# Two preparation stages in a chunked delta net: masked scores two blocks ahead, decays and inverses one block ahead

## The chip, the cores and the metric

One core of a Trainium2 chip runs the whole kernel. The metric is the device time of one execution in microseconds; the table below gives the median of three runs. TensorE does the matmuls, VectorE and ScalarE the work on PSUM and SBUF, GpSimd the products that need no PSUM, SyncE issues the transfers.

## The reference

Two layers run over 1040 tokens of 1024 features: a gated delta net, a gated feed-forward layer with a causal convolution, an mLSTM and a second feed-forward layer, each between root-mean-square norms. The change touches the gated delta net only. For each of 16 value heads (two to each of 8 query/key heads) and each chunk it computes

```python
G = cumsum(g)                                   # g: log decays of a chunk
decay = exp(where(i >= j, G[i] - G[j], -inf))
a_mat = I + (beta*k) @ k.T * decay * strict     # strict: below the diagonal
u, w = solve(a_mat, [v*beta, k*beta*exp(G)])
attn = (q @ k.T) * decay
# from chunk to chunk, S the state of a head:
v_new = u - w @ S
o = (q*exp(G)) @ S + attn @ v_new
S = S*exp(G_last) + (k*exp(G_last - G)).T @ v_new
```

Here q and k are the outputs of a projection, a causal convolution of four taps and a SiLU, then divided by their norms; o is normed, multiplied by a gate z, and projected back.

## The kernel before, in words

**Tiling.** The tokens lie along the free dimension, 1044 with padding: three token blocks of 348 (`BS`), each of three chunks of 116 (`CH`). Features lie on the 128 partitions. The delta net walks through 24 blocks, n = 3h + b for query/key head h and token block b. A block has two value heads.

**Projections.** A unit is one tile of 128 output features for one token block: eight k-steps of three matmuls each (`mm3`: high weight by high input, high by low, low by high), 24 matmuls of 128x348. `project(n)` makes two tiles for all three token blocks, six units, 144 matmuls. It yields in the middle and at the end of each unit, so it has twelve steps. With n mod 3 = 0 it makes the two z tiles of head h, with 1 the q and k tiles of head h + 1, with 2 the two v tiles of head h + 1, and ends with a burst of SiLUs on ScalarE between two loads of activation tables. Each unit of q, k or v also has a convolution: a multiply by the norm's factors (L308), one ScalarE pass (L695) and three VectorE passes (L697).

**Preparation** (`gdn_prepare`, L738). First the scores, three steps: the squares of k (L746), their sum over features by two matmuls (`kn`, L274 and L275), its inverse root, k times that (L750); k against k, masked, into `scs_kk`; k against q, masked, into `scs_qk` (`score_block`, L576 and L579, one buffer each). Then for each of the two value heads the decays (`decay_block`: transposed sums L559, `eG` L561, `E` L566 and L567), the masked matrix `ah` (L911) with its rest `A` and `al` on GpSimd (L914, L915), its first level (L912), `att` (L764) and the decayed q (`qd`, L767) on GpSimd. The tiles eG, E and A share three buffers. Then the two inverses in step with each other: Z (L920), X by TensorE (L923) and ScalarE (L924), six doubling levels of three steps each (L949, L958, L963 with L953, L959, L964), a correction (L969 to L977) and the result XT (L979).

**Recurrence** (`gdn_recur`) goes through a block's three chunks with the state S: k, v0 and v1 transposed (L795), k by S (L828), XT by the difference (L839), the new state (L848, L854) and, one chunk later, the outputs (L812, L813). **Finish** (`gdn_finish`) norms and gates a block's outputs and stores them.

**Order.** The kernel is written as generators. `weave` takes steps from several of them in proportion to weights: next comes the one with the smallest (steps done + 0.5) / weight. One `weave` is made for each block n, and the next starts in the program's order only when all its parts are done. The order so written is a priority: a planner orders each engine's instructions by readiness under its own estimates of durations, earlier written ones first, and gives out buffers as it goes. On the chip each engine then runs its own list in that fixed order, with semaphores between engines.

```python
            parts = [(self.gdn_recur(n, tb), 14)]
            if n + 1 < n_all:
                parts.insert(0, (self.gdn_prepare(n + 1, tb, lb), 27))
            if n:
                parts.append((self.gdn_finish(n - 1), 4))
            parts.append((project(n), 8) if n <= n_all - NB else (islice(out, 28), 28))
            weave(*parts)
```

So the preparation of block n + 1, scores included, stands beside the recurrence of block n. The projection has twelve steps at weight 8, so that when the other parts have reached their ends some four of its steps are left. In the last two blocks the steps of the output projection (`out`) take its place.

Of the kernel before, what the change touches and what calls it, by code (L numbers as in the profile page):

```python
# [23 lines left out]
NB = 3  # L24
# [40 lines left out]
def weave(*parts):  # L65

    live = [[g, max(n, 1), 0] for g, n in parts]
    while live:
        p = min(live, key=lambda p: (p[2] + 0.5) / p[1])
        try:  # L70
            next(p[0])
            p[2] += 1
        except StopIteration:
            live.remove(p)


def run(g):
    for _ in g:
        pass


class Trunk:
# [154 lines left out]
    def project(self, w, b, name, rows=P):  # L237

        ps = self.next_bank(f"pj_{name}_{b}")
        for k in range(KD):  # L240
            self.mm3(ps[:rows, :BS], w[k], self.x(k, b), k == 0, k == KD - 1)
        if self.now:
            self.now.pop()()
        return ps[:rows, :BS]
# [361 lines left out]
    def gdn(self):  # L606
        a = self.a
        self.o_dram = [self.pd.tile([P, 2, TP], F32, tag=f"o_g_{h}", name=f"o_g_{h}", bufs=1) for h in range(NQK)]
        self.pages_of = {}
        self.blocks = {}  # L610
        n_all = NQK * NB
        tiles = lambda h: [h, NQK + h, 2 * NQK + 2 * h, 2 * NQK + 2 * h + 1, 32 + 2 * h, 32 + 2 * h + 1]

        def silu(h, tiles):
            self.burst([y for i in tiles for y in self.pages_of[h, i]], self.last, AF.Silu)

        def project(n):


            h, part = divmod(n, NB)  # L620
            i = (4, 0, 2)[part]
            g = h + (part > 0)
            yield from self.gdn_project(g, tiles(g)[i : i + 2], i)
            silu(g, (i, i + 1))

        def enter(b):
            hs = []
            for m in range(KD):
                h = self.page("C", f"hs_in_{b}_{m}", N_PAGES)
                sl = slice(b * BS, (b + 1) * BS)  # L630
                nc.sync.dma_start(h, self.hs[:, m, sl])
                self.put_input(h, m, sl)
                hs.append(h)
            return hs

        nc = self.nc
        t0 = tiles(0)
        weights = lambda t: self.split_weights(a["gdn_w_in"][t], f"gi{t}")
        self.new_input(0, "in")
        self.rt = self.new_factors("in")  # L640
        wg = self.split_weights(a["gdn_gate_w"], "gdn_gates", 32)
        hs = [enter(0)]
        ws = [weights(t0[0])]
        self.tables()
        hs.append(enter(1))
        ws.append(weights(t0[1]))
        hs.append(enter(2))
        rows = []
        for b in range(NB):
            acc = self.squares(hs[b], f"in{b}")  # L650
            self.now.append(lambda acc=acc, b=b: self.norm(acc, f"in{b}", self.r(b)))
            rows.append(self.gate_rows(wg, b, "gdn"))
            if b == NB - 1:
                gates = self.gdn_gates(rows)
                next(gates)
            for i in range(2):
                run(self.gdn_unit(0, i, t0[i], ws[i], b))
        lb, tb = next(gates)
        silu(0, (0, 1))
        order = t0[2:4] + [t for h in range(NQK) for t in tiles(h)[4:] + (tiles(h + 1)[:4] if h + 1 < NQK else [])]  # L660
        self.queue_weights([(a["gdn_w_in"][t], f"gi{t}") for t in order], 1)

        def first():
            yield from self.gdn_project(0, tiles(0)[2:4], 2)
            silu(0, (2, 3))

        weave((self.gdn_prepare(0, tb, lb), 13), (first(), 6))
        out = self.out_projection(a["gdn_w_out"], NQK, "go", GDN_CORE, GDN_LATE, 1, 2)
        for n in range(n_all):
            parts = [(self.gdn_recur(n, tb), 14)]  # L670
            if n + 1 < n_all:
                parts.insert(0, (self.gdn_prepare(n + 1, tb, lb), 27))
            if n:
                parts.append((self.gdn_finish(n - 1), 4))
            parts.append((project(n), 8) if n <= n_all - NB else (islice(out, 28), 28))
            weave(*parts)
        weave((self.gdn_finish(n_all - 1), 4), (out, 30))

# [56 lines left out]
            reason="issue order",  # L735
        )

    def gdn_prepare(self, n, tb, lb):  # L738


        nc, core = self.nc, self.core
        h, b = divmod(n, NB)
        q, k = self.pages_of[h, 0][b], self.pages_of[h, 1][b]
        nm = f"{h}_{b}"
        ksq = self.scratch(f"ksq_{nm}")
        nc.scalar.activation(ksq, k, AF.Square)  # L746
        ps = self.bank("sp", f"kn_{nm}")
        self.over_features(ps[:, :BS], ksq, f"k{nm}")
        rk = self.rstd(ps[:, :BS], 1.0, EPS, f"k{nm}")
        nc.vector.tensor_tensor(k, k, rk, ALU.mult)  # L750
        yield
        kk = self.score_block(k, k, self.m_strict, f"kk{nm}")
        yield
        qk = self.score_block(k, q, self.m_incl, f"qk{nm}")
        yield
        at, qd, invs = [], [], []
        XT = [None, None]
        for i in range(2):
            vh = 2 * h + i
            E, eG = self.decay_block(tb, lb, vh, b, f"{vh}_{b}")  # L760
            invs.append(self.inverse(kk, E, f"{vh}_{b}", i, XT))
            next(invs[i])
            att = core.tile([CH, BS], F32, tag="att", name=f"att_{vh}_{b}", bufs=4)
            nc.gpsimd.tensor_tensor(att, qk, E, ALU.mult)  # L764
            at.append(att)
            qe = core.tile([P, BS], F32, tag="qd", name=f"qd_{vh}_{b}", bufs=4)
            nc.gpsimd.tensor_tensor(qe, q, eG, ALU.mult)  # L767
            qd.append(qe)
            yield
        while invs:  # L770
            for g in list(invs):
                if next(g, 1):
                    invs.remove(g)
            yield
        self.blocks[n] = (at, qd, XT)
# [722 lines left out]
```

## Time and profile before

| | |
|---|---|
| median of 3 runs | 3444.45 us (3444.33 to 3444.45) |
| time of the profiled execution | 3444.23 us |
| its span | 3442.5 us |
| mean granted TensorE clock | 0.969 |
| TensorE busy (matmuls) | 3212.2 us, 93% of the span |
| VectorE busy | 2373.1 us, 69% |
| ScalarE busy | 1609.0 us, 47% |
| GpSimd busy | 1652.2 us, 48% |

The span runs from the first to the last instruction. Matmuls are pipelined and their ends are modelled in the profile, so a busy TensorE is not one at its peak; how far apart matmuls start says more. PE stands for TensorE, PEld for its weight loads, DVE for VectorE, ACT for ScalarE, POOL for GpSimd. A row of a group or of the timeline ends with the idle time of the engine just before it and the instruction that ended that idle time. The granted clock is the share of full speed that TensorE was given.

### The profile page before, as it was taken

The numbers are of one execution on the slowest core, as the hardware profiler recorded it, in microseconds if no ns is written. First come the engines' busy times: TensorE is split into PE (matmuls) and PEld (weight loads), VectorE is DVE, ScalarE is ACT, GpSimd is POOL, SyncE is SP. The second block draws the span as 40 slices with busy tenths as digits, with TensorE's granted clock in tenths as the row PEclk, the third lists the DMA queues.
The fourth block names the chain that finished last, engine by engine and source line by source line (L and its number), as shares of the span: only waits on it lengthen the run. The fifth ranks groups of instructions, "written<-read, shape, count | busy, mean of one in ns | idle before, by whom it ended". The sixth has DMA issues, their size and how long they took to land. (4 is left out here: it accounts for less than half of the span.)

```text
span 3442.5 us, 68429 instructions
## 1 busy us (share of the span) xinstructions
PE 3212.2 (93%) x25368; PEld 3119.6 (91%) x25368; DVE 2373.1 (69%) x5143; ACT 1609.0 (47%) x3390; POOL 1652.2 (48%) x1890
## 2 busy tenths in 40 slices
PE   7999999999999998799999989899998799999998
PEld 6889988988988897799999989899998799999998
DVE  7777777777767649877677484534469867777474
ACT  5455545555545435655455243323345645445232
POOL 2433443444334444577665434333344477666453
PEclk9999999999999999899999999999999899999999
DMA  3011100101001344422224453211125422224452
GB/s 118 23 37 34 34 29 31 34 32 34 31 31 40 107 132 152 134 93 93 78 78 133 133 182 125 93 44 50 56 78 183 136 90 87 87 75 132 132 180 88
DMA packets 234511, 297.75 MB, mean 86 GB/s; under 512 B 20684, under 2 KB 167104, under 8 KB 234176
## 3 DMA queue, kind: packets, MB, share of 16 engines
q1 hardware_dynamic: 234176, 293.37, 26.3%
q8 instruction: 200, 3.28, 0.4%
q14 instruction: 135, 1.11, 0.1%
HBM read 240.06 MB, written 53.23 MB: 85 GB/s over the span
## 5 line engine op out<-in xcount | busy, mean ns | idle before, releaser
L233 PE MATMUL pj_gi<-xh_in,wh_gi 128*128 128x348 f32 x1152 | 394.2, 342 | 5.5 <-ACT wh_gi L137 3.7
L233 PE MATMUL dn_f<-so_f,wh_f 128*128 128x260 f32 x1344 | 386.6, 288 | 11.8 <-ACT wh_f L137 5.0
L235 PE MATMUL pj_gi<-xh_in,wl_gi 128*128 128x348 f32 x1152 | 395.7, 343 | 0.9 <-POOL wl_gi L138 0.9
L234 PE MATMUL pj_gi<-xl_in,wh_gi 128*128 128x348 f32 x1152 | 393.5, 342 | 0.0
L235 PE MATMUL dn_f<-so_f,wl_f 128*128 128x260 f32 x1344 | 384.7, 286 | 0.0
L234 PE MATMUL dn_f<-so_f,wh_f 128*128 128x260 f32 x1344 | 384.5, 286 | 0.0
L138 POOL TENSOR_TENSOR wl_f<-wr_f,wh_f 128x512 fp32r<-128x512 f32 x168 | 226.0, 1362 | 246.0 <-ACT wh_f L137 113.5
L1278 DVE SCALAR_TENSOR_TENSOR z<-u,fcw,z 128x260 f32<-128x260 f32 x528 | 243.4, 487 | 49.8 <-ACT z L1276 35.0
L138 POOL TENSOR_TENSOR wl_u_s<-wr_u,wh_u_s 128x512 fp32r<-128x512 f32 x176 | 228.2, 1300 | 97.7 <-ACT wh_u_s L137 97.3
L233 PEld LDWEIGHTS dn_f<-so_f,wh_f 128*128 128x128 f32 x1344 | 257.7, 192 | 13.6 <-ACT z L1276 5.5
L441 DVE TENSOR_TENSOR acc_f<-acc_f,dn_f 128x260 f32<-128x260 f32 x320 | 133.1, 421 | 189.2 <-PE dn_f L235 188.2
L234 PEld LDWEIGHTS dn_f<-so_f,wh_f 128*128 128x128 f32 x1344 | 258.2, 192 | 0.2
L235 PEld LDWEIGHTS dn_f<-so_f,wl_f 128*128 128x128 f32 x1344 | 258.2, 192 | 0.1
L1276 ACT ACTIVATE z<-u,fcb,fcw 128x260 f32<-128x260 f32 x352 | 192.3, 570 | 93.7 <-DVE u L196 92.4
L233 PEld LDWEIGHTS pj_gi<-xh_in,wh_gi 128*128 128x128 f32 x1152 | 222.1, 193 | 8.0 <-ACT wh_gi L137 4.0
L235 PEld LDWEIGHTS pj_gi<-xh_in,wl_gi 128*128 128x128 f32 x1152 | 222.6, 193 | 2.4 <-POOL wl_gi L138 1.2
L234 PEld LDWEIGHTS pj_gi<-xl_in,wh_gi 128*128 128x128 f32 x1152 | 222.2, 193 | 0.7 <-issue 0.2
L138 POOL TENSOR_TENSOR wl_gi<-wr_gi,wh_gi 128x512 fp32r<-128x512 f32 x96 | 132.4, 1380 | 157.8 <-ACT wh_gi L137 153.8
L137 ACT CAST wh_u_s<-wr_u 128x512 fp32r<-128x512 f32 x176 | 105.9, 615 | 192.5 <-PE up L234 134.9
L697 DVE SCALAR_TENSOR_TENSOR gy<-u_g,c_gdn_conv_w_g,gy 128x348 f32<-128x348 f32 x288 | 187.9, 663 | 7.9 <-ACT gy L695 5.4
L138 POOL TENSOR_TENSOR wl_u_a<-wr_u,wh_u_a 128x512 fp32r<-128x512 f32 x132 | 170.1, 1293 | 37.0 <-ACT wh_u_a L137 36.3
L137 ACT CAST wh_f<-wr_f 128x512 fp32r<-128x512 f32 x168 | 103.1, 617 | 178.8 <-PE dn_f L234 133.0
(501 smaller groups left out, 11718.0 us busy)
## 6 DMA issues: line engine op xcount, KB each, us to landing
wr_u<-in_ffn_w_up_dram SPq DMA_DIRECT2D x224, 256.0 KB, 2.6
wr_f<-in_ffn_w_down_dram SPq DMA_DIRECT2D x176, 256.0 KB, 2.8
wr_gi<-in_gdn_w_in_dram SPq DMA_DIRECT2D x96, 256.0 KB, 2.6
h<-y SPq DMA_DIRECT2D x176, 130.0 KB, 2.3
si_f<-h SPq DMA_DIRECT2D x88, 260.0 KB, 3.5
wr_go<-in_gdn_w_out_dram SPq DMA_DIRECT2D x64, 256.0 KB, 2.7
wr_mi<-in_ml_w_in_dram SPq DMA_DIRECT2D x44, 256.0 KB, 2.6
o_g<-gy SPq DMA_DIRECT2D x48, 174.0 KB, 1.8
```

The lines of the kernel that those rows point to most:

```text
L137: nc.scalar.copy(hi, part(raw))
L138: nc.gpsimd.tensor_tensor(lo, part(raw), hi.bitcast(F32), ALU.subtract)
L233: nc.tensor.matmul(out, w[0], x[0], start=start, stop=False)
L234: nc.tensor.matmul(out, w[0], x[1], start=False, stop=False)
L235: nc.tensor.matmul(out, w[1], x[0], start=False, stop=stop)
L441: nc.vector.tensor_tensor(acc[m][n], acc[m][n], ps, ALU.add)
L697: ins = nc.vector.scalar_tensor_tensor(y, u[:, j : j + BS], taps[:, j : j + 1], y, ALU.mult, ALU.add)
L1276: nc.scalar.activation(z, p[:, 2 : 2 + QB], AF.Identity, scale=taps[:, 2:3], bias=self.fcb[:, tt : tt + 1])
L1278: nc.vector.scalar_tensor_tensor(z if i or not h else y[h], p[:, i : i + QB], taps[:, i : i + 1], z, ALU.mult, ALU.add)
```

## The change

The first part of the preparation becomes a generator of its own, `gdn_scores(n)`: norm of k, the two masked score blocks, three steps. `gdn_prepare(n)` takes the two from a dictionary and starts with the decays. Beside block n now stand the decays and inverses of block n + 1 (weight 24) and the scores of block n + 2. The scores wait six steps at weight 9 before their first one, so that they come in the last part of the block, when `scs_kk` and `scs_qk` of block n + 1 have been read. Where block n + 2 opens a head, its q and k come out of this block's projection; there the scores are put behind the projection in one generator of fifteen steps, weight 15. Elsewhere the projection has weight 12. Before block 0 stand the scores and the preparation of block 0 and the scores of block 1.

```diff
-        self.blocks = {}
+        self.blocks, self.scores = {}, {}
...
-        weave((self.gdn_prepare(0, tb, lb), 13), (first(), 6))
+        def ahead():
+            yield from self.gdn_scores(0)
+            yield from self.gdn_prepare(0, tb, lb)
+            yield from self.gdn_scores(1)
+
+        def scores(n, wait):
+
+            for _ in range(wait):
+                yield
+            yield from self.gdn_scores(n)
+
+        def project_and_scores(n):
+            yield from project(n)
+            yield from self.gdn_scores(n + 2)
+
+        weave((ahead(), 30), (first(), 12))
         out = self.out_projection(a["gdn_w_out"], NQK, "go", GDN_CORE, GDN_LATE, 1, 2)
         for n in range(n_all):
             parts = [(self.gdn_recur(n, tb), 14)]
             if n + 1 < n_all:
-                parts.insert(0, (self.gdn_prepare(n + 1, tb, lb), 27))
+                parts.insert(0, (self.gdn_prepare(n + 1, tb, lb), 24))
             if n:
                 parts.append((self.gdn_finish(n - 1), 4))
-            parts.append((project(n), 8) if n <= n_all - NB else (islice(out, 28), 28))
+            if n + 2 < n_all and n % NB != 1:
+                parts.append((scores(n + 2, 6), 9))
+            if n > n_all - NB:
+                parts.append((islice(out, 28), 28))
+            elif n % NB == 1:
+
+                parts.append((project_and_scores(n), 15))
+            else:
+                parts.append((project(n), 12))
             weave(*parts)
...
-    def gdn_prepare(self, n, tb, lb):
-
+    def gdn_scores(self, n):
...
         qk = self.score_block(k, q, self.m_incl, f"qk{nm}")
         yield
+        self.scores[n] = kk, qk
+
+    def gdn_prepare(self, n, tb, lb):
+
+        nc, core = self.nc, self.core
+        h, b = divmod(n, NB)
+        q = self.pages_of[h, 0][b]
+        kk, qk = self.scores.pop(n)
         at, qd, invs = [], [], []
```

## The prediction

> **What bounds the kernel now.** I read the page first, then the waits of TensorE inside the delta net's stage, then one block's timeline, then busy time by stretch, and last the heads against each other.
>
> ```profile
> span 3442.5 us, 68429 instructions
> PE 3212.2 (93%) x25368; PEld 3119.6 (91%) x25368; DVE 2373.1 (69%) x5143; ACT 1609.0 (47%) x3390; POOL 1652.2 (48%) x1890
> ```
>
> TensorE is busy for 93% of the span, so a change of order can only win back TensorE's losses. The delta net is the stretch from about 80 to 1220 us; the change touches nothing outside it. These are the waits of TensorE there (total us, times, longest):
>
> ```profile
> PE px L923 <- DVE Z L920: 46.5, 40, 2.7
> PE S L848 <- DVE E L566: 10.0, 14, 0.9
> ...
> PE kn L275 <- DVE al_k L273: 2.5, 6, 0.4
> ...
> PE row L559 <- DVE scs_qk L579: 1.4, 6, 0.2
> ...
> PE sc_kk L576 <- DVE gy L750: 1.1, 1, 1.1
> ```
>
> The first two rows are the opening of the inverses (the masked matrix, its first level and Z) and the decays. Only the last three, 2.5 + 1.4 + 1.1 = 5.0 us, belong to the score steps that move. One block in order of time, VectorE's rows with one of TensorE's:
>
> ```profile
> 656.57 0.52 DVE L979 SCALAR_TENSOR_TENSOR XT<-Z,px_f 116x348 f32<-116x348 f16 x1 [0.32 <-PE px_f L977]
> 667.75 0.52 DVE L579 TENSOR_TENSOR scs_kk<-sc_kk,c_m_strict_g 116x348 f32<-116x348 f32 x1 [1.45 <-PE sc_kk L576]
> 668.36 0.52 DVE L579 TENSOR_TENSOR scs_qk<-sc_qk,c_tri_g 116x348 f32<-116x348 f32 x1
> 670.58 0.70 DVE L566 TENSOR_SCALAR E<-row,dt_s_gdn,gd_lb 116x116 f32<-116x116 f32 x2 [0.20 <-ACT eG L561]
> 672.58 0.60 DVE L911 TENSOR_TENSOR ah<-scs_kk,E 116x348 f16<-116x348 f32 x1 [0.56 <-ACT E L567]
> 675.00 1.01 DVE L566 TENSOR_SCALAR E<-row,dt_s_gdn,gd_lb 116x116 f32<-116x116 f32 x3 [0.83 <-POOL att L764]
> 675.93 0.91 DVE L920 TENSOR_TENSOR Z<-l,i 116x348 f16<-116x348 f16 x1
> 676.90 0.37 PE L923 MATMUL px<-i,Z 116*116 116x116 f16 x3 [1.49 <-DVE Z L920]
> 698.20 0.51 DVE L979 SCALAR_TENSOR_TENSOR XT<-Z,px_f 116x348 f32<-116x348 f16 x1
> ```
>
> The preparation of this block runs from the last inverse at 656.57 to its own last inverse at 698.20: about 12 us until the scores stand, 4 us of decay, 26 us of inverses. TensorE's hold-up is at 676.90: Z stands in VectorE's queue behind the second head's E, and that E waits 0.83 us for GpSimd to finish att. Now one head by stretch, first the score and decay stretches of its three blocks, then the inverse stretches (columns: us, PE, PEld, DVE, ACT, POOL busy, granted clock, DMA):
>
> ```profile
> 656.60:672.10 15.50, 15.06 (x103) 14.50 (x102) 9.55 (x20) 9.38 (x18) 3.77 (x5) 1.00 0.11 35
> 698.20:712.00 13.80, 13.77 (x93) 13.27 (x92) 7.29 (x19) 9.25 (x18) 4.98 (x8) 1.00 0.13 45
> 745.10:764.20 19.10, 18.87 (x124) 18.16 (x123) 14.66 (x29) 12.68 (x24) 9.34 (x11) 1.00 0.17 52
> ...
> 672.10:698.20 26.10, 24.11 (x241) 22.82 (x240) 20.20 (x55) 12.06 (x31) 10.33 (x11) 1.00 0.06 21
> 712.00:745.10 33.10, 29.89 (x269) 28.15 (x268) 27.60 (x68) 13.50 (x34) 13.20 (x18) 0.95 0.07 24
> 764.20:793.00 28.80, 26.91 (x261) 25.56 (x260) 24.25 (x64) 14.16 (x36) 13.36 (x17) 1.00 0.09 31
> ```
>
> So while the score chain runs, TensorE is 97 to 99% busy: the trailing projection covers that chain. The losses lie in the inverse stretches (90 to 93% busy), and the least busy of them, 29.89 of 33.10 us, is where the granted clock fell to 0.95. The projection's matmuls in these three inverse stretches, by their tile:
>
> ```profile
> 672.10:698.20 26.10, 14.27 (x58) 9.09 (x57) 1.03 (x2) 1.00 0.06 21
> 712.00:745.10 33.10, 17.97 (x75) 12.25 (x74) 1.55 (x3) 0.95 0.07 24
> 764.20:793.00 28.80, 15.89 (x71) 10.83 (x70) 1.54 (x3) 1.00 0.09 31
> ```
>
> Of a block's 144 projection matmuls (two tiles, three token blocks, eight k, three products) only 58 to 75 stand beside the inverses. Last, five heads, each from the square of its first block's keys to the next head's:
>
> ```profile
> 342.10:483.10 141.00, 133.23 (x1080) 127.04 (x1080) 103.56 (x247) 70.97 (x159) 54.92 (x68) 0.95 0.09 31
> 483.10:618.00 134.90, 127.08 (x1082) 121.18 (x1081) 103.48 (x247) 71.13 (x161) 55.48 (x68) 1.00 0.10 33
> 618.00:754.30 136.30, 128.55 (x1080) 122.37 (x1080) 103.54 (x247) 70.97 (x159) 54.95 (x68) 0.99 0.10 32
> 754.30:890.70 136.40, 128.60 (x1081) 122.50 (x1080) 103.56 (x247) 71.08 (x161) 55.46 (x68) 0.99 0.10 32
> 890.70:1031.80 141.10, 133.32 (x1081) 127.21 (x1080) 103.49 (x247) 71.01 (x159) 55.38 (x68) 0.95 0.10 31
> ```
>
> The same work takes 134.9 us at full clock and up to 141.1 where the clock dropped.
>
> **The change part by part.** No arithmetic is added or removed, no DMA is issued by the moved steps, and nothing of them goes to GpSimd or SyncE; those queues only see the projection's weight splits earlier within a block. The sum is made against the profiled span of 3442.5 us; its execution took 3444.23 us, 0.22 us under the median of the runs.
>
> *The score steps* (four ScalarE, four VectorE and fourteen TensorE instructions a block) move from the head of their block's preparation into the last part of the block before. What covered them was trailing projection; now it is the evenly spread one, and in every third block, where the scores follow the projection that makes their keys, the next block's. Their own TensorE waits are 5.0 us. I take half away, -2.5; the ends are -5.0 (all gone) and +5.0 (each wait doubled beside the denser work). If their cover failed, the price would be the 12 us chain a block; the 97 to 99% busy rows say it is covered, so the shortened chain itself is worth nothing.
>
> *The opening of the inverses* keeps its order: E of head 0, att, E of head 1, Z. The wait on att comes of the three shared buffers of E, eG and A and of GpSimd's order, and neither is edited. I take 0. The bounds come from the 46.5 + 10.0 = 56.5 us: -28 if the projections ranked ahead in the even spread fill half of those waits, +28 if the opening, no longer behind a quiet stretch, meets half as much again.
>
> *The projection's weight, 8 to 12 (15 with scores behind it).* Before, eight of twelve half units keep pace with the rest of a block and four trail, 48 matmuls. Now all keep pace, so the inverse stretches get thicker with projection. That has two prices. The first is that each return from small matmuls to the projection costs extra:
>
> ```profile
> 772.67 0.30 PE L958 MATMUL px<-pl,Z 116*116 116x58 f16 x3
> 772.81 0.41 PE L234 MATMUL pj_gi<-xl_in,wh_gi 128*128 128x348 f32 x1
> 773.06 0.32 PE L235 MATMUL pj_gi<-xh_in,wl_gi 128*128 128x348 f32 x1
> 773.21 0.32 PE L233 MATMUL pj_gi<-xh_in,wh_gi 128*128 128x348 f32 x1
> 773.37 0.29 PE L949 MATMUL pp<-X,ah 116*116 116x58 f16 x3
> ```
>
> The first matmul of a run holds the engine for 0.25 us (772.81 to 773.06), the following ones 0.15 to 0.16: 0.09 us a return. With 42 groups of the two inverses a block (twenty-one steps, two heads) returns could rise by some fifteen a block if every group stood alone, or fall by four if the heads' groups pair up. Over 23 blocks that is +31 or -8 us. I take two more a block, 23 x 2 x 0.09 = +4, near the present pairing since the two heads' steps still issue together.
>
> The second is the clock. Against the 134.9 us head the others lose 6.1, 1.4, 1.5 and 6.2, together 15.2 us in five heads. The drop came in the stretch with the least TensorE work, and that is the stretch that gets a part of the 48 trailing matmuls. I take most of it away, -11; the ends are -15 and +6 (one more head hit as the worst are). The Trainium skill's page "TensorE: Matmul & The Clock Gate", section "HAM oscillation — how this bites in real kernels", puts the condition for a throttled clock as idle gaps of TensorE above some 3.4 us. By that rule these drops have no cause in the stage, whose longest wait of the inverses is 2.7 us; the trace shows drops all the same, and if the rule held, this term would be 0 and the result the first rival's.
>
> *The last head.* Block 22's opening, where the projection is over and the output projection starts:
>
> ```profile
> 1111.00:1135.00 24.00, 16.88 (x107) 14.56 (x106) 15.00 (x32) 15.19 (x30) 10.68 (x12) 0.86 0.38 119
> ```
>
> 7.1 us are idle there. Block 23's scores now come one block earlier, but the output projection's own operands stay late: -2, ends -7 and +2. The start-up weave only renames its ratio (13 to 6 against 30 to 12): 0.
>
> Sum: -2.5 + 0 + 4 - 11 - 2 = -11.5 us, so 3431 for the span and **3433 us** for the runs.
>
> **The rivals.** *No change that can be measured* (0.2%, about 7 us, is what this kernel's measurement can tell): the score chain is hidden already, so shortening it frees nothing, and the clock drops follow from something other than the thin stretch. For it: TensorE's 97 to 99% during the chain. Against it: of the three inverse stretches shown, the 0.95 is that of the thinnest. Without the -11 the sum is -0.5: 3444 us. This is also the case in which the planner had already ordered things as the change asks.
>
> *Slower, by the opening.* Today the opening follows a stretch with VectorE 53 to 77% and GpSimd 24 to 49% busy. After the change it follows straight on the previous block's inverses, with conv, weight splits and the finishing multiplications in the same two queues. E of head 1 and Z then come later, and TensorE, whose order is fixed, stands at L923 longer. Today's price is 56.5 / 24 = 2.4 us a block; half as much again is +28 and gives 3461 us. It decides from 0.5 us more a block (11.5 / 23), and shows as slower from 0.8. Against it: VectorE was 77 to 84% busy in the stretch where the opening falls now, so the mean load there may even fall.
>
> *Clearly faster, by the same place.* If the planner puts the projections that now rank ahead of L923 into those waits, half of the 56.5 us goes: 3433 - 28 = 3405 us. Against it: projection matmuls stand ready today too, and still the wait is there.
>
> **How the numbers follow.** Forecast (its own range 3424 to 3438) 0.36, no change 0.24, slower 0.22, clearly faster 0.18. The range takes in both outer rivals, 3403 to 3461. Faster: 0.18 and nearly all of 0.36 make 0.52; within 0.2%: 0.25; slower: 0.23.
>
> **What would show it.** The decays of a block right behind the last inverse instead of 14 us later, and scs_kk ahead of that inverse; granted clock 1.00 in third blocks; L923's wait still 40 to 55 us in total. The prediction is wrong if L923's wait moves by more than a third, if heads at full clock take other than 133 to 137 us, or if a new wait appears on scores in the blocks that open a head.

## The result, and the profile after

The changed kernel takes 3469.56 us (median of 4 runs, 3467.24 to 3470.59) against 3444.45 us: 1.0067 times as long by the means of four executions each, 95% interval 1.0050 to 1.0085. That is slower, outside the range given and on the other side of the forecast. The profiled execution, 3469.0 us, has this page:

```profile
span 3467.2 us, 68290 instructions
...
PE 3225.1 (93%) x25368; PEld 3125.1 (90%) x25368; DVE 2388.0 (69%) x5143; ACT 1604.6 (46%) x3390; POOL 1657.8 (48%) x1890
```

The counts of each engine are those of before, so the 24.7 us of span are an effect of order alone. The last inverse of block 23 ends at 1203.1 us instead of 1184.9, so 18.2 us come in the delta net. The other 6.5 come behind it, 3.2 of them in the kernel's last 140 us, where the change does nothing; no run here explains the 6.5.

TensorE's waits from 80 to 1250 us, the changed kernel (total us, times, longest):

```profile
PE w L869 <- DVE E L566: 19.7, 8, 4.5
PE px L953 <- DVE Z L950: 17.1, 26, 1.6
PE S L878 <- DVE wv L871: 10.8, 7, 1.6
PE row L559 <- DVE E L566: 10.8, 8, 1.5
PE ks L858 <- DVE St L881: 6.3, 7, 0.9
PE w L869 <- DVE r L862: 4.4, 7, 0.6
```

The wait at Z (line 953 now, 923 before) fell from 46.5 to 17.1 us. In its place TensorE stands in the recurrence (w, S, ks) and at the decays' transposes (row). All rows of that answer together rose from 74.1 to 86.3 us. Five heads of the changed kernel, cut like the heads of before:

```profile
339.80:479.20 139.40, 130.12 (x1081) 123.04 (x1080) 105.33 (x247) 70.48 (x160) 56.26 (x68) 0.99 0.10 32
479.20:619.80 140.60, 130.35 (x1081) 123.12 (x1080) 106.65 (x247) 70.66 (x160) 56.31 (x68) 0.99 0.10 31
619.80:759.10 139.30, 129.99 (x1081) 122.89 (x1080) 105.34 (x247) 70.42 (x159) 56.26 (x68) 0.99 0.09 32
759.10:899.60 140.50, 130.20 (x1081) 123.03 (x1080) 106.67 (x247) 70.61 (x160) 56.32 (x68) 0.99 0.10 31
899.60:1039.10 139.50, 130.20 (x1081) 123.12 (x1080) 105.43 (x247) 70.58 (x161) 56.30 (x68) 0.99 0.10 32
```

The clock is steadier: 0.99 in every head, no more 0.95. Yet each head takes 139 to 141 us, where before a head at 0.99 took 136.3 and one at 1.00 took 134.9. So 3 to 4 us a head were lost to something else than the clock. Here is the longest single wait in these heads, VectorE and then TensorE (the recurrence's rows) in the opening of the block that starts a head:

```profile
629.57 0.50 DVE L308 TENSOR_TENSOR u_g<-pj_gi,r_in 128x348 f32<-128x348 f32 x1
630.00 0.81 DVE L273 TENSOR_TENSOR al_o<-osq,ah_o 128x348 fp32r<-128x348 f32 x1
630.73 1.60 DVE L941 TENSOR_TENSOR ah<-scs_kk,E 116x348 f16<-116x348 f32 x1
632.25 0.34 DVE L862 SCALAR_TENSOR_TENSOR r<-ks,dt_nE_gdn,vt 116x128 f32<-116x128 f32 x1
632.52 0.81 DVE L942 TENSOR_TENSOR l<-ah,c_m_g 116x348 f16<-116x348 f16 x1
634.13 1.01 DVE L566 TENSOR_SCALAR E<-row,dt_s_gdn,gd_lb 116x116 f32<-116x116 f32 x3 [0.81 <-POOL att L794]
635.06 0.91 DVE L950 TENSOR_TENSOR Z<-l,i 116x348 f16<-116x348 f16 x1
635.89 0.34 DVE L862 SCALAR_TENSOR_TENSOR r<-ks,dt_nE_gdn,vt 116x128 f32<-116x128 f32 x1
```

```profile
629.47 0.48 PE L559 MATMUL row<-c_ident_g,dt_G_gdn 116*128 116x116 f32 x3
629.78 0.61 PE L858 MATMUL ks<-St,gy 128*116 128x256 f32 x2
635.29 0.45 PE L869 MATMUL w<-r,XT 116*116 116x128 f32 x2 [2.18 <-DVE E L566]
636.45 0.38 PE L869 MATMUL w<-r,XT 116*116 116x128 f32 x2
```

The recurrence's two r, one for each value head, stand 3.6 us apart in VectorE's queue. Between them lie the first level, the wait on att with head 1's E, and Z. The first w needs only the first r, which is done at 632.59. Yet it starts at 635.29, right behind E, which ends at 635.14. The source points to the reason: the norms, the scores, row, tr, ks, w, S and the outputs all take their PSUM buffer from one tag, `sp`, with two buffers.

```python
    def bank(self, tag, name):
        return self.ps.tile([P, 512], F32, tag=tag, name=name, bufs=2)
```

In TensorE's order the row of head 1, ks and w follow each other. So w takes the buffer of that row, and head 1's E is the last to read it. E in turn waits for att, and GpSimd comes late to att. E of head 0 is ready at 630.20, but a weight split of the projection (`wl_gi`) stands ahead of A and att:

```profile
630.43 1.52 POOL L138 TENSOR_TENSOR wl_gi<-wr_gi,wh_gi 128x512 fp32r<-128x512 f32 x1
631.91 1.21 POOL L944 TENSOR_TENSOR A<-scs_kk,E 116x348 f32<-116x348 f32 x1
633.09 1.01 POOL L794 TENSOR_TENSOR att<-scs_qk,E 116x348 f32<-116x348 f32 x1
```

With the projection's weight at 8 (x1_weight8, the first experiment below) no split stands there; E of head 0 is ready at 622.64 and A starts at once:

```profile
622.72 1.44 POOL L944 TENSOR_TENSOR A<-scs_kk,E 116x348 f32<-116x348 f32 x1 [0.73 <-ACT E L567]
```

```profile
626.34 0.45 PE L869 MATMUL w<-r,XT 116*116 116x128 f32 x2 [0.77 <-DVE E L566]
```

A starts 1.71 us behind E of head 0 in the changed kernel and 0.08 at weight 8; w waits 2.18 us and 0.77. It is so in all seven blocks that open a head, with waits of 2.16 to 2.20 us and 0.76 to 0.79. No run gave `sp` a third buffer or took the split out of that place alone.

### The profile page after: what moved, and what is told of

Read it like the earlier page. It is cut to its first block, busy times and chain, and to the rows that moved or that the text cites. A ratio compares the mean times of both kernels' runs of the same rounds, so it can differ in the third digit from the quotient of the medians.

```text
span 3467.2 us, 68290 instructions
## 1 busy us (share of the span) xinstructions
PE 3225.1 (93%) x25368; PEld 3125.1 (90%) x25368; DVE 2388.0 (69%) x5143; ACT 1604.6 (46%) x3390; POOL 1657.8 (48%) x1890
```

## The experiments

Ratios are against the kernel before in the same job, with the 95% interval. "Five heads" is the stretch from the inverse of block 6 to that of block 21, in each kernel's own trace. In all these traces the granted clock is either full or half; how long it stood at half is taken from the traces' clock records. The first theory (A) was that the opening now collides with the recurrence's first steps because it stands at the head of the block; the rival (B), that the projection's weight does it.

**The weight back at 8** (x1_weight8), the split kept.

```diff
-                parts.append((project_and_scores(n), 15))
+                parts.append((project_and_scores(n), 10))
             else:
-                parts.append((project(n), 12))
+                parts.append((project(n), 8))
```

> The changed kernel with the projection's weight back at 8 (10 with scores behind it): scores still two blocks ahead, decays and inverses still at the head of a block. Theory A, the opening of the inverses now stands in VectorE's queue beside the recurrence's first steps: nothing of that is undone, 3462 to 3475 us, and TensorE's waits at the recurrence's w, S and ks and at row stay near 45 us. Theory B, the evenly spread projection costs it (more returns to the projection, no dense stretch left): back to 3440 to 3452 us.

3440.15 us, 0.9979 (0.9966 to 0.9991), 29 us under the changed kernel. Theory B's time came, A's did not. Of B's reasons the returns are small: 86 a head here and 94 in the changed kernel, 8 x 0.09 = 0.7 us. TensorE's waits over five heads, this kernel (its five longest rows):

```profile
PE px L953 <- DVE Z L950: 18.5, 25, 2.4
PE sc_kk L576 <- DVE gy L772: 5.2, 5, 1.0
PE w L869 <- ACT gy L718: 4.4, 5, 0.9
PE w L869 <- DVE E L566: 3.8, 5, 0.8
PE row L559 <- DVE E L566: 3.0, 5, 0.6
```

and the changed kernel's:

```profile
PE w L869 <- DVE E L566: 10.9, 5, 2.2
PE px L953 <- DVE Z L950: 10.8, 17, 1.0
PE S L878 <- DVE wv L871: 7.7, 5, 1.6
PE row L559 <- DVE E L566: 7.4, 5, 1.5
PE ks L858 <- DVE St L881: 4.5, 5, 0.9
PE w L869 <- DVE r L862: 3.1, 5, 0.6
PE tr L825 <- ACT gy L747: 2.0, 5, 0.4
PE w L869 <- DVE ktb L827: 1.1, 2, 0.6
```

At weight 8 the recurrence's waits are 8.2 us, at 12 they are 29.3 (its w, S, ks and tr rows).

**Weight 12 in the kernel before.**

```diff
-            parts.append((project(n), 8) if n <= n_all - NB else (islice(out, 28), 28))
+            parts.append((project(n), 12) if n <= n_all - NB else (islice(out, 28), 28))
```

> The kernel before with the projection's weight at 12 and nothing else. Theory A: 3438 to 3450 us, since scores still stand ahead of the decays and keep the opening away from the recurrence's start. Theory B: most of the loss appears here too, 3458 to 3470 us, with more returns from small matmuls to the projection than 88 a head.

3454.99 us, 1.0024 (1.0010 to 1.0037): between both expectations. The weight costs 8 us here against 29 in the split kernel, so it is not the weight alone. The returns rose to 94 a head, as theory B had it. Over five heads the time itself does not show the loss, 688.0 us against 689.7 before. The clock hides it: it stood at half for 14 us of them instead of 34, some 10 us if half of that time counts as lost. The same kind of wait appears; its rows over five heads:

```profile
PE px L923 <- DVE Z L920: 19.2, 20, 1.9
PE ks L828 <- DVE scs_kk L579: 9.7, 10, 1.6
PE tr L795 <- DVE wv L841: 6.6, 5, 1.3
PE S L848 <- DVE E L566: 4.8, 5, 1.0
```

**A later opening** (x3_late) at weight 12: six empty steps ahead of the decays.

```diff
-                parts.insert(0, (self.gdn_prepare(n + 1, tb, lb), 24))
+                parts.insert(0, (late(n + 1), 30))   # six yields, then gdn_prepare
```

> The changed kernel with six empty steps ahead of the decays (weight 30 for 30 steps), so that the opening of the inverses comes a fifth of a block later, as it did before, with the scores still two blocks ahead and the projection at 12. Theory A: the loss goes, 3435 to 3450 us, waits at w, S, ks and row down to under 25 us in total. Theory B: 3462 to 3475 us.

3480.47 us, 1.0086 (1.0065 to 1.0108): above both expectations. The recurrence's waits did fall to 23.2 us, as theory A had it; the clock took more than that gain. It stood at half for 61 us of the five heads, against 17 in the changed kernel. So A's time did not come, but its mechanism is not refuted. Why the clock fell is not shown. Five heads by busy time (us, PE, PEld, DVE, ACT, POOL, clock, DMA):

```profile
381.80:1095.00 713.20, 670.37 (x5397) 631.95 (x5396) 530.60 (x1237) 354.62 (x796) 272.24 (x341) 0.96 0.09 31
```

**Weight 10.** The edit is that of weight 8 with 10 and 12.5.

> The changed kernel with the projection's weight at 10 (12.5 with scores behind it), between 8 and 12. Theory C, with a higher weight GpSimd's weight splits, the finishing steps and the convolutions of the block crowd into the opening of the inverses: in between, 3448 to 3462 us. Rival theory D, the time hangs on how the planner's order happens to fall and not on the weight as such: outside the stretch from 3440 to 3470 us, or no better than 3465 us.

3448.78 us, 1.0009 (0.9990 to 1.0028). In the split kernel weights 8, 10 and 12 give 3440, 3449 and 3469 us. The times rise with the weight, as theory C had it, and theory D's ranges did not come. The step from 8 to 10 is the less certain one: the two intervals touch, the ten executions at 10 lie between 3437.5 and 3464.4 us, and the profiled ones took 684.3 us over five heads at 8 and 682.3 at 10. The clock stood at half for 20 us of the first and never in the second. Three points do not rule out that other accidents of order have a part.

**Only two of three blocks at 8** (x13_p8_s15), and 15 kept where the scores stand behind the projection.

```diff
             elif n % NB == 1:
                 parts.append((project_and_scores(n), 15))
             else:
-                parts.append((project(n), 12))
+                parts.append((project(n), 8))
```

> The changed kernel with the projection's weight at 8 in two of three blocks, and the 15 kept only in the block where the scores stand behind the projection. If that one block carries the loss (its projection must be through at 12/15 of the block): 3460 to 3472 us. If the loss lies in the other two: 3438 to 3446 us. If each block carries its share: 3446 to 3458 us, with the recurrence's waits over five heads between 8 and 29 us.

3472.28 us, 1.0078 (1.0061 to 1.0095): as slow as the changed kernel, just above the first range. Against weight 8 everywhere, the only difference is 15 or 10 in the block that projects the next head's q and k. At 15 the projection must be through at 12/15 of the block and the scores behind it at its end; at 10 the projection's last two steps and the scores come behind the block's other parts. TensorE's waits over five heads:

```profile
PE px L953 <- DVE Z L950: 16.4, 23, 1.0
PE w L869 <- DVE E L566: 11.0, 5, 2.2
PE row L559 <- DVE E L566: 9.8, 5, 2.1
PE S L878 <- DVE wv L871: 4.7, 3, 1.6
PE w L869 <- DVE r L862: 3.1, 5, 0.6
```

The 2.2 us at w and the waits at row are back, each once a head, and so is the weight split ahead of A. But the loss is made up otherwise than in the changed kernel:

```profile
380.50:1092.80 712.30, 666.78 (x5397) 635.78 (x5397) 525.90 (x1236) 352.12 (x796) 278.10 (x341) 0.95 0.09 31
```

The clock stood at half for 68 us of these five heads, against 20 at weight 8 and 17 in the changed kernel. If half of that time is taken as lost, an estimate, the five heads without it take 678 us here, 674 at weight 8 and 691 in the changed kernel. So the 15 in this one block costs as much as the whole change, mostly by the clock. That the changed kernel, which kept its clock, loses its time in this block is not shown by it.

**The projection's first third ahead of everything** (x9_front). Four of its steps are written before the block's weave, the rest at 8.

```diff
+            if n <= n_all - NB:
+                run(islice(ahead_of, 4))   # ahead_of: project(n), with scores where n % NB == 1
...
-                parts.append((project(n), 12))
+                parts.append((ahead_of, 8))
```

> The changed kernel with the first four of the projection's twelve steps written ahead of everything else in a block, and the other eight beside the rest at weight 8 (11 with scores behind them). A dense stretch stands again at the block's border as with weight 8, but of this block's projection and not of the one before. Theory C (what counts is what stands beside the opening and after it): 3436 to 3450 us. If it is the trailing, so that the block's last units lie outside the block, that helps: 3455 to 3472 us.

3509.92 us, 1.0181 (1.0165 to 1.0198), outside both expectations. A dense stretch at the block's border is not enough to help; with projection ranked ahead of the chain this is the slowest of all. The clock stood at half for 102 us of the five heads:

```profile
391.80:1125.50 733.70, 677.73 (x5397) 645.04 (x5396) 530.97 (x1236) 351.19 (x795) 272.06 (x339) 0.93 0.09 30
```

**Finishing held back**, then **the recurrence at weight 20**, both at weight 12.

```diff
-                parts.append((self.gdn_finish(n - 1), 4))
+                parts.append((late_finish(n - 1), 8))   # four yields, then gdn_finish
```

> The changed kernel (projection 12) with the finishing of block n - 1 held back by four empty steps (weight 8 for eight steps), so that its GpSimd and VectorE instructions leave the opening of the inverses. If it is these that crowd the opening at weight 12: 3450 to 3460 us, TensorE's waits in the recurrence over five heads from 29 to under 15 us. If the convolutions and weight splits of the projection do it: 3463 to 3475 us and the recurrence's waits stay above 22 us.

3475.13 us, 1.0107 (1.0062 to 1.0152), at the upper end of the second range. The recurrence's waits rose to 40.2 us over five heads, so holding the finishing steps back does not free the opening.

```diff
-            parts = [(self.gdn_recur(n, tb), 14)]
+            parts = [(self.gdn_recur(n, tb), 20)]
```

> The changed kernel (projection 12) with the recurrence's weight at 20 instead of 14, so that its steps rank ahead of more of the projection and of the opening. If the recurrence's waits come of its place in the order: they fall under 15 us over five heads, 3450 to 3462 us. If VectorE is slowed as such at weight 12 (its busy time over five heads 529 us against 515 to 518 at weight 8): the waits move back to Z, 3463 to 3480 us.

3477.85 us, 1.0090 (1.0075 to 1.0106). The recurrence's waits fell to 13.4 us, as the first expectation had it, and the time did not: Z rose to 27.0 and row to 12.4 us. VectorE's busy time was 510 us, so it was not slow as such either. The time lies in the second range, but that range's reason did not hold. Here the waits moved from one chain to the others.

**Four buffers for E, eG and A**, one more than before: in the changed kernel, in the kernel before, and at weight 8.

```diff
-        E = self.core.tile([CH, BS], F32, tag="e", name=f"E_{name}", bufs=3)
+        E = self.core.tile([CH, BS], F32, tag="e", name=f"E_{name}", bufs=4)   # so for eG, A, grow; tail: 6 to 5
```

> The changed kernel with four shared buffers for E, eG and A instead of three (and five small buffers for convolution tails instead of six, to make room). Head 1's E no longer has to wait for GpSimd's att. Theory A in its narrow form, that this wait is what holds VectorE's queue: 3448 to 3460 us. If the queue is only full of slow instructions and this wait is a small part of it, or by theory B: 3464 to 3472 us.

> The kernel before with four shared buffers for E, eG and A. Its VectorE waited 12.5 us for att in all, and TensorE stood 46.5 us at Z behind that: theory C 3432 to 3441 us. If these waits only shift to the next instruction in VectorE's queue: 3442 to 3448 us.

> Weight 8 as in x1_weight8, and four shared buffers for E, eG and A (convolution tails five). If the wait on att costs the same at either weight, the 11 us of x4_e4 come on top: 3425 to 3434 us. By theory C GpSimd is pressed less at weight 8, so there is less to win: 3434 to 3441 us.

3458.31 us, 1.0031 (1.0020 to 1.0042) for the changed kernel; 3424.59, 0.9930 (0.9913 to 0.9946) for the one before; 3414.69, 0.9908 (0.9894 to 0.9923) at weight 8. The first lies in its first range, near the upper end; the other two are faster than both of their ranges. VectorE's wait for att that this takes away was, without the fourth buffer, in the changed kernel

```profile
DVE E L566 <- POOL att L794: 6.5, 8, 0.8
```

and at weight 8

```profile
DVE E L566 <- POOL att L794: 18.3, 22, 0.9
```

with 12.5 us in the kernel before. The gains are 11 us in the changed kernel, 25 at weight 8 and 22 in the kernel before, larger than the waits taken away. TensorE's wait at Z fell in all three. The clock over five heads rose from 0.98 to 1.00 in the kernel before and from 0.99 to 1.00 at weight 8, the two that gained most; in the changed kernel it fell from 0.99 to 0.98. Five heads at weight 8 with four buffers run at full clock:

```profile
366.00:1030.10 664.10, 634.19 (x5398) 606.81 (x5397) 517.94 (x1237) 355.68 (x796) 279.37 (x341) 1.00 0.10 33
```

The expectation that there is less to win at weight 8 was wrong: there is most.

**Weight 6 with four buffers** (7.5 with scores).

> The changed kernel with four shared buffers and the projection's weight at 6 (7.5 with scores behind it). If a lower weight goes on helping below 8: 3402 to 3411 us. If 8 is low enough that the projection already ranks behind the chain: 3411 to 3420 us. If too little projection is left beside the inverses: 3420 to 3440 us with a granted clock below 1.00 again.

3411.71 us, 0.9900 (0.9881 to 0.9918), in the second range by 0.7 us, and not told apart from weight 8 with four buffers. Both beat the kernel before and the changed one.

## Why the prediction was wrong, by its steps

The measured 25 us slower stands against a forecast of 11.5 us faster.

*The score steps, -2.5.* The size came out, partly by luck. Of their 5.0 us of waits 2.5 are left (0.9 at sc_kk, 1.6 at row behind scs_kk), but both fall at 96 and 100 us, in the start-up, which was taken as 0. In the five heads none of these rows is left, where 3.2 us stood before.

*The opening, taken as 0.* This is the step that failed. Its argument was that the order E, att, E, Z is not edited. It is not, but I priced only who stands before Z and not who stands behind the same VectorE instructions or waits for the PSUM buffer that E still has to read. Z's own wait fell by 29 us, more than the -28 of the faster bound and far beyond the third that was named as a sign of being wrong. Behind Z and E, the recurrence's w, r, wv and St and the next transposes were late, and TensorE's waits as a whole rose by 12 us. My rival "slower, by the opening" had the place. That its 3461 us came near was luck: its +28 was to come at L923, whose wait fell. It gave the cause to an opening that follows straight on the last block; in x3_late, where it comes later, the recurrence's waits fell by only 6 us of 29 and the kernel was slower still. GpSimd's queue, which it named among the crowded ones, held the longest wait.

*The projection's weight, taken for its returns and the clock.* The returns went as sized: counted in the trace, 88 a head before and 94 after, 6 x 8 x 0.09 = 4 us. The clock's term was right in kind: the heads at 0.95 are gone. It stood at half for 34 us of the five heads before and for 17 after. If half of that is lost, an estimate, the change saved about 9 us of the 11 taken. The clock went down to 0.93 in x9_front, where TensorE's longest wait in the five heads was 2.8 us. The rule that I had weighed, from the Trainium skill's page "TensorE: Matmul & The Clock Gate", section "HAM oscillation — how this bites in real kernels", ties the drop to idle gaps of TensorE above some 3.4 us. These runs do not agree with it as the only condition. What I left out of this term weighed most: with the weights at 8 and 10, x1_weight8, the loss is gone and the split wins 0.2%. The weight does not only spread the matmuls; it also puts the projection's weight splits ahead of the opening's products on GpSimd. With 15 in one block of three it forces the projection of q and k, its convolutions and the scores to be through by the block's end. x13_p8_s15 shows that the 15 alone costs as much as the change did, though there mostly by the clock.

*The accounting.* Five heads took 699.2 us after and 689.7 before: +9.5. By the clock that is about -9, by TensorE's waits +8.8 (47.5 against 38.7). The remaining 9 to 10 us lie almost all inside TensorE's busy time, which was 650.8 us in both although the clock was better after. The returns account for 2.7 of them (6 x 5 x 0.09); the rest no run explains. The stretch before block 6 cost another 5.4 us, with the clock at 0.97 against 0.99, the last head 3.3 where I had taken -2, and the part behind the delta net 6.5. I had a term for none of these but the last head.

*The range.* Its upper end was the rival's 3461, a sum that still contained the whole gain of the clock. The changed kernel kept the gain and paid more than that rival.

What stays open is how the loss divides among the queues. The weight split ahead of A accounts for most of the difference at `w <- E`, 10.9 us over five heads at weight 12 against 3.8 at 8. Three ways to move the waits at weight 12 (a later opening, later finishing, an earlier recurrence) shifted them and made the kernel slower, so no single queue is shown to be the cause of the whole. Nor is it shown what lets the clock fall in x3_late, x9_front and x13_p8_s15.

## What to carry to other kernels

When engines run fixed lists and TensorE is 93% busy, a step moved off a chain that was covered anyway can win little: here the moved waits were 5.0 us in all. What counts is which chain is then last in the shared queue, so price everyone who stands behind the moved instructions or waits for a buffer that they hold. Independent bulk work did best here where it ranked behind the latency chain and filled its holes: the median rose from 8 to 10 to 12, while 6 was no better than 8. Compare the time lost to waits and the time lost to the clock separately, since two orders equally slow can lose it in different ways. Look first for a short wait of one engine for a buffer in the middle of a queue: one more buffer in the kernel before was worth 22 us here, the best split without it 7.

## What the runs showed of the hardware

The clock fell without long waits. Without a wait of even 3 us in the five heads, the granted clock was 0.93 with 55.9 us of TensorE waits (x9_front), 0.98 with 38.7 (before) and 1.00 with 29.6 (weight 8, four buffers); it was also 1.00 with 43.7 at weight 10 and 0.95 with 45.0 in x13_p8_s15, so the sum of the waits alone does not set it. And one and the same VectorE instruction, the product `ah`, took 0.51 us at its fastest and 1.61 at its slowest in the changed kernel, with a mean of 1.11 us over the five heads against 0.88 before and 0.70 at weight 8. No run isolates the reason.
